# Row-wise sum of reciprocals: larger loads first, smaller loads last, and one layout of two-row chunks

## The chip, the core and the metric

The kernel runs on one core of a Trainium2 chip. The metric is the device time of one execution in microseconds (us); before the change it is 175.22 us, the median of 3 runs (174.59 to 175.49). The profile is of one execution whose span, from the first to the last instruction, is 172.6 us.

The engines are named as in the profile: PE is TensorE's matmul, PEld its weight load, DVE is VectorE, ACT is ScalarE, POOL is GpSimd, SP is SyncE, on whose queue all loads are issued here.

## What is computed

```python
x: 32 x 512 x 1024, float32, positive
return np.sum(1.0 / x, axis=-1)
```

There are 16384 rows of 1024 values. Each of the 128 partitions gets 128 consecutive rows, so in a partition the rows lie one behind the other in HBM, 4 KB each. In all 67.11 MB are read and 64 KB are written.

## The kernel before

No engine divides here. Each row is cut into halves a and b of 512 values, and the kernel uses

1/a + 1/b = (a + b) / (a b).

The reciprocal of a product is computed on ScalarE as exp(-ln(S a b)), with the constant S = 2^17 in front, which is multiplied in again at the end. This needs a logarithm and an exponential for 512 values where a row taken alone would need both for 1024.

The work is cut into groups of one or two rows (`GROUPS`, L38-L44). For each group the loop at L80 does the following.

- A load brings the group's rows into a tile xt (L82-L83). xpool has 16 such tiles of two rows. All loads are on SyncE's queue.
- The product pr = a b is formed on GpSimd (L85); in the very last group it is formed on VectorE.
- In groups marked `on_pe` (B in the code), TensorE forms the sum a + b in PSUM (L90): a matmul with an identity matrix for a, and a second one for b that is accumulated onto it. The tile is sm.
- ScalarE takes the logarithm of pr (L106) and then the exponential (L111), in place in groups B, and into a PSUM tile rc in the others (A).
- VectorE multiplies and sums in one instruction (L118). In a group A it multiplies the whole row (1024 values) by rc, which is used for both halves; in a group B it multiplies the reciprocal (512 values) by the sum in sm. An accumulator is read into `sums` after it (DVE_READ_ACCUMULATOR2).
- A group C has one row like A and a second row that ScalarE does alone: logarithm and exponential of 1024 values with the sum in its accumulator (L98, L99). There are seven such groups.

The last six groups have one row each. The order of the work on each engine is that of the framework's scheduler. At the end the 64 KB of sums are stored with one DMA (L131).

A tile goes back to its pool when the last instruction that reads or writes it has ended. In a group A that is VectorE's sum, which reads xt; in a group B the tile xt is free once GpSimd and TensorE have read it.

Of the kernel before, what the change touches and what calls it, by code (L numbers as in the profile page):

```python
# [1 line left out]

# [6 lines left out]


@with_exitstack
def kernel(
    ctx: ExitStack,
    tc: tile.TileContext,
    x: bass.AP,
    out: bass.AP,
):

    nc = tc.nc
    f32 = mybir.dt.float32
    P = 128
    D = 1024
    H = D // 2  # L30
    F = 128

    S = float(2**17)

    GP, DV = nc.gpsimd, nc.vector
    A, B, C = (2, 0, GP, False), (2, 0, GP, True), (1, 1, GP, False)  # L38
    GROUPS = (
        [A, B, A, B, C, B, A, B] * 7  # L40
        + [A, B, A, B, A]
        + [(1, 0, GP, True), (1, 0, GP, False)] * 2
        + [(1, 0, GP, True), (1, 0, DV, True)]
    )  # L44

    Ln = mybir.ActivationFunctionType.Ln
    Exp = mybir.ActivationFunctionType.Exp
    mult = mybir.AluOpType.mult
    add = mybir.AluOpType.add

    x_v = x.flatten_outer_dims().rearrange("(p f) d -> p f d", p=P)
    out_v = out.flatten().rearrange("(p f) -> p f", p=P)

    act_sets = list(get_activation_tables(nc.m.arch).keys())
    nc.scalar.add_instruction(  # L55
        mybir.InstLoadActFuncSet(
            name=nc.get_next_instruction_name(),
            act_func_set_id=act_sets.index("natural_log_exp_and_others"),
            ins=[],
            outs=[],  # L60
        )
    )

    xpool = ctx.enter_context(tc.tile_pool(name="xpool", bufs=16))
    ppool = ctx.enter_context(tc.tile_pool(name="ppool", bufs=4))
    opool = ctx.enter_context(tc.tile_pool(name="opool", bufs=1))
    rpool = ctx.enter_context(
        tc.tile_pool(name="rpool", bufs=2, space=bass.MemoryType.PSUM)
    )

    spool = ctx.enter_context(
        tc.tile_pool(name="spool", bufs=2, space=bass.MemoryType.PSUM)
    )

    sums = opool.tile([P, F], f32)
    ident = opool.tile([P, P], f32)
    make_identity(nc, ident)

    c0 = 0
    for np_, ns, eng, on_pe in GROUPS:  # L80
        n = np_ + ns
        xt = xpool.tile([P, n, D], f32, tag="xt")  # L82
        nc.sync.dma_start(out=xt, in_=x_v[:, c0 : c0 + n, :])  # L83
        pr = ppool.tile([P, np_, H], f32, tag="pr")
        eng.tensor_tensor(out=pr, in0=xt[:, :np_, :H], in1=xt[:, :np_, H:], op=mult)  # L85
        if on_pe:
            sm = spool.tile([P, np_, H], f32, tag="sm")
            for j in range(np_):
                for h in range(2):
                    nc.tensor.matmul(  # L90
                        sm[:, j, :],
                        lhsT=ident,
                        rhs=xt[:, j, h * H : (h + 1) * H],
                        start=h == 0,
                        stop=h == 1,
                    )
        for j in range(np_, n):
            nc.scalar.activation(out=xt[:, j, :], in_=xt[:, j, :], func=Ln)  # L98
            nc.scalar.activation(  # L99
                out=xt[:, j, :],  # L100
                in_=xt[:, j, :],
                func=Exp,
                scale=-1.0,
                accum_out=sums[:, c0 + j : c0 + j + 1],
            )
        nc.scalar.activation(out=pr, in_=pr, func=Ln, scale=S)  # L106
        if on_pe:
            rc = pr
        else:
            rc = rpool.tile([P, np_, H], f32, tag="rc")  # L110
        nc.scalar.activation(out=rc, in_=pr, func=Exp, scale=-1.0)  # L111
        for j in range(np_):
            if on_pe:
                row, rec = rc[:, j, :], sm[:, j, :]
            else:
                row = xt[:, j, :].rearrange("p (h e) -> p h e", h=2)
                rec = rc[:, j, :].unsqueeze(1).to_broadcast([P, 2, H])
            nc.vector.tensor_tensor_reduce(  # L118
                out=row,
                in0=row,  # L120
                in1=rec,
                scale=S,
                scalar=0.0,
                op0=mult,
                op1=add,
                accum_out=sums[:, c0 + j : c0 + j + 1],
            )
        c0 += n
    assert c0 == F, c0

    nc.sync.dma_start(out=out_v, in_=sums)  # L131


# [1 line left out]
_INS = ['x']  # L135
_OUTS = [((32, 512), 'float32')]


# [23 lines left out]
```

## Time and profile before

| | us | share of the span |
|---|---|---|
| device time | 175.22 | |
| span of the profiled execution | 172.6 | |
| POOL busy | 143.4 | 83% |
| ACT busy | 142.0 | 82% |
| PE busy | 120.9 | 70% |
| DVE busy | 109.8 | 64% |

| operation | line | count | mean of one |
|---|---|---|---|
| POOL product, two rows (128x1024) | L85 | 54 | 2365 ns |
| POOL product, one row (128x512) | L85 | 12 | 1273 ns |
| ACT logarithm, two rows | L106 | 54 | 1055 ns |
| ACT exponential into PSUM, two rows (A) | L111 | 24 | 1027 ns |
| ACT exponential in place, two rows (B) | L111 | 30 | 1056 ns |
| DVE sum of a whole row (A) | L118 | 57 | 1219 ns |
| DVE sum of a half row (B) | L118 | 64 | 685 ns |
| DVE product of one row | L85 | 1 | 689 ns |

The busy times and shares come from the first part of the page. Matmuls are counted twice there: each of the 128 in the program shows as two passes. A busy share says little by itself: the table only says that no compute engine is busy throughout. The slices, the chain and the waits say what the time is spent on; they are shown with the prediction. A group's mean in the second table is for one shape alone.

### The profile page before, as it was taken

Reading aid. Unit: us, or ns where it says so; the run is one execution under the profiler, and the core shown is the slowest. Engines: PE = TensorE matmul, PEld = TensorE weight load, DVE = VectorE, ACT = ScalarE, POOL = GpSimd, SP = SyncE. Lnnn points to the kernel's source line nnn. Section 1 sums busy time; section 2 is a strip of 40 time slices with the busy share of each in tenths; the row PEclk is TensorE's granted clock in tenths of the full one; section 3 lists DMA queues with packets and bytes.
Section 4 is the critical chain, followed back from the end, with each engine's and each line's share of the span. In section 5 each row is a group of like instructions: output and inputs, shape, how many; then the busy total and the mean of one; then the engine's idle time right before and its main releaser. Section 6 shows DMA issues by size and latency. Waiting matters only on the chain.

```text
span 172.6 us, 1342 instructions
## 1 busy us (share of the span) xinstructions
PE 120.9 (70%) x256; PEld 47.4 (27%) x256; DVE 109.8 (64%) x243; ACT 142.0 (82%) x156; POOL 143.4 (83%) x72
## 2 busy tenths in 40 slices
PE   0099776767876767788666668977667876669480
PEld 0043322222332222233322223422222332223130
DVE  0009757874776757775578847468576755787791
ACT  2159989899878998889888996889988898988981
POOL 1599699969989799987999688997999979999920
PEclk9999999999999999999999996999999999999999
DMA  5999999999999999999999999999999999999500
GB/s 190 416 433 425 423 420 423 421 421 423 418 425 420 423 418 423 423 420 423 421 421 420 423 414 423 421 420 420 425 418 425 425 420 421 421 412 408 220 0 15
DMA packets 9799, 67.25 MB, mean 390 GB/s; under 512 B 1088, under 2 KB 1216, under 8 KB 1984
## 3 DMA queue, kind: packets, MB, share of 16 engines
q1 hardware_dynamic: 9792, 67.18, 94.0%
q8 instruction: 2, 0.03, 0.1%
q14 instruction: 5, 0.04, 0.1%
HBM read 67.11 MB, written 0.07 MB: 389 GB/s over the span
## 4 chain that ended last, share of the span: by engine, by line
DMA 78%; POOL 11%; ACT 2%; issue 2%; DVE 2%; SPq 1%; PE 1%; POOLq 0%; DVEq 0%
DMA xt<-in_x_dram 78%; POOL pr L85 11%; SPq L83 1%; ACT pr L106 1%; PE sm L90 1%; DVE xt L118 1%; ACT rc L111 1%; DVE pr L118 0%; ACT pr L111 0%; DVE pr L85 0%; POOLq L85 0%; DVE sums L118 0%; DVEq L118 0%; DVEq L157 0%
## 5 line engine op out<-in xcount | busy, mean ns | idle before, releaser
L85 POOL TENSOR_TENSOR pr<-xt 128x1024 f32<-128x1024 f32 (+1 forms) x66 | 142.7, 2166 | 21.1 <-DMA xt<-in_x_dram 15.2
L90 PE MATMUL sm<-xt,ident 128*128 128x512 f32 x256 | 120.9, 617 | 47.0 <-DMA xt<-in_x_dram 45.0
L118 DVE CUSTOM_DVE_ANT_1 xt<-xt,rc 128x1024 f32<-128x1024 f32 x57 | 67.7, 1219 | 50.2 <-issue 27.2
L106 ACT ACTIVATE pr<-pr 128x1024 f32<-128x1024 f32 (+1 forms) x67 | 65.0, 970 | 24.5 <-POOL pr L85 23.7
L90 PEld LDWEIGHTS sm<-xt,ident 128*128 128x128 f32 x256 | 47.4, 195 | 119.7 <-issue 57.8
L118 DVE CUSTOM_DVE_ANT_0 pr<-pr,sm 128x512 f32<-128x512 f32 x64 | 41.6, 685 | 9.8 <-ACT pr L111 8.6
L111 ACT ACTIVATE pr<-pr 128x1024 f32<-128x1024 f32 (+1 forms) x34 | 34.2, 1006 | 1.0
L111 ACT ACTIVATE rc<-pr 128x1024 f32<-128x1024 f32 (+1 forms) x33 | 29.9, 906 | 0.8
L118 DVE DVE_READ_ACCUMULATOR2_ANT sums<- 128x1 f32 x121 | 10.0, 82 | 0.0
L99 ACT ACTIVATE xt<-xt 128x1024 f32<-128x1024 f32 x7 | 7.3, 1041 | 0.0
L98 ACT ACTIVATE xt<-xt 128x1024 f32<-128x1024 f32 x7 | 7.3, 1040 | 0.0
L55 ACT ACT_TABLE_LOAD x1 | 1.3, 1283 | 0.7 <-PEq L146 0.7
L99 ACT ACTIVATION_READ_ACCUMULATOR xt<-xt 128x1 f32 x7 | 1.3, 186 | 0.0
L85 DVE TENSOR_TENSOR pr<-xt 128x512 f32<-128x512 f32 x1 | 0.7, 689 | 0.0
masks.py:197 POOL MEMSET ident<- 128x128 f32 x1 | 0.2, 204 | 0.3 <-POOLq L146 0.3
masks.py:199 POOL TENSOR_SCALAR_AFFINE_SELECT ident<-ident 128x128 f32<-128x128 f32 x1 | 0.3, 292 | 0.1
L146 POOL MEMSET const-float32-0.0<- 128x1 f32 x1 | 0.1, 98 | 0.2 <-issue 0.2
L146 POOL MEMSET const-bfloat16-1.0<- 128x1 bf16 x1 | 0.1, 101 | 0.0
L146 POOL MEMSET const-uint8-127<- 128x1 uint8 x1 | 0.1, 101 | 0.0
L146 POOL MEMSET const-float32-1.0<- 128x1 f32 x1 | 0.1, 98 | 0.0
## 6 DMA issues: line engine op xcount, KB each, us to landing
xt<-in_x_dram SPq DMA_DIRECT2D x61, 1024.0 KB, 19.8
xt<-in_x_dram SPq DMA_DIRECT2D x6, 512.0 KB, 15.6
out_dram<-sums SPq DMA_DIRECT2D x1, 64.0 KB, 1.5
```

Of the source, the lines that this page charges most:

```text
L55: nc.scalar.add_instruction(mybir.InstLoadActFuncSet(name=nc.get_next_instruction_name(), act_func_set_id=act_sets.index("natural_log_exp_ ...
L83: nc.sync.dma_start(out=xt, in_=x_v[:, c0 : c0 + n, :])
L85: eng.tensor_tensor(out=pr, in0=xt[:, :np_, :H], in1=xt[:, :np_, H:], op=mult)
L90: nc.tensor.matmul(sm[:, j, :], lhsT=ident, rhs=xt[:, j, h * H : (h + 1) * H], start=h == 0, stop=h == 1,)
L98: nc.scalar.activation(out=xt[:, j, :], in_=xt[:, j, :], func=Ln)
L99: nc.scalar.activation(out=xt[:, j, :], in_=xt[:, j, :], func=Exp, scale=-1.0, accum_out=sums[:, c0 + j : c0 + j + 1],)
L106: nc.scalar.activation(out=pr, in_=pr, func=Ln, scale=S)
L111: nc.scalar.activation(out=rc, in_=pr, func=Exp, scale=-1.0)
L118: nc.vector.tensor_tensor_reduce(out=row, in0=row, in1=rec, scale=S, scalar=0.0, op0=mult, op1=add, accum_out=sums[:, c0 + j : c0 + j + 1],)
L146: nc = _bacc.Bacc("TRN2", target_bir_lowering=False, num_devices=1)
```

## The change

The change replaces the mixture of groups by chunks of two rows and takes several chunks with one load.

- A load brings eight rows (8 loads), then four rows (12 loads), then two rows (8 loads): 28 loads in place of 67. Per partition a load is one run of 32, 16 or 8 KB. The large tiles come from xpool (4 tiles of eight rows), the two-row tiles from a pool of their own, epool (4 tiles).
- All chunks have two rows. A is as before. B has the halves added on TensorE, as before. C is like B, but the product of its first row is formed on VectorE, from b as TensorE has copied it to PSUM (a matmul with the identity) and a in SBUF. C is every fourth chunk, so this is every eighth product. No row is done on ScalarE alone any more.
- The order on each engine is fixed to that of the program (`keep`). The sums of a chunk are issued one chunk later (`waiting`), behind the products of the next chunk. A C chunk's product on VectorE stands at the head of its load.
- The pools change: ppool has 6 tiles for 4. In PSUM there are three tiles of one row for the sums, one for b, and two of two rows for rc.

It is meant to have fewer and longer transfers, shares that suit the engines, and short pieces at the end.

```diff
-    A, B, C = (2, 0, GP, False), (2, 0, GP, True), (1, 1, GP, False)
-    GROUPS = (
-        [A, B, A, B, C, B, A, B] * 7
-        + [A, B, A, B, A]
-        + [(1, 0, GP, True), (1, 0, GP, False)] * 2
-        + [(1, 0, GP, True), (1, 0, DV, True)]
-    )
+    A, B, C = (2, 0, 0), (2, 2, 0), (2, 2, 1)
+    LOADS = [[A, B, A, C]] * 8 + [[A, B], [A, C]] * 6 + [[A], [B], [A], [C]] * 2
...
-    xpool = ctx.enter_context(tc.tile_pool(name="xpool", bufs=16))
-    ppool = ctx.enter_context(tc.tile_pool(name="ppool", bufs=4))
+    xpool = ctx.enter_context(tc.tile_pool(name="xpool", bufs=4))
+    epool = ctx.enter_context(tc.tile_pool(name="epool", bufs=4))
+    ppool = ctx.enter_context(tc.tile_pool(name="ppool", bufs=6))
...
+    for chunks in LOADS:
+        n = sum(m for m, _, _ in chunks)
+        if n > 2:
+            xt = xpool.tile([P, n, D], f32, tag="xt")
         else:
+            xt = epool.tile([P, n, D], f32, tag="xe")
+        keep(nc.sync.dma_start(out=xt, in_=x_v[:, c0 : c0 + n, :]))
+
+        made, q = [], 0
+        for m, e, v in chunks:
+            pr = ppool.tile([P, m, H], f32, tag="pr")
+            for j in range(v):
+                b = bpool.tile([P, H], f32, tag="b")
+                add(b, xt[:, q + j, H:])
+                i = nc.vector.tensor_tensor(
+                    out=pr[:, j, :], in0=xt[:, q + j, :H], in1=b, op=mult
+                )
+                keep(i)
...
+        for (m, e, v), pr in zip(chunks, made):
+            xc = xt[:, q : q + m, :]
+            if v < m:
+                i = nc.gpsimd.tensor_tensor(
+                    out=pr[:, v:, :], in0=xc[:, v:, :H], in1=xc[:, v:, H:], op=mult
+                )
+                keep(i)
+            sm = []
+            for j in range(e):
+                s = spool.tile([P, H], f32, tag="s")
+                add(s, xc[:, j, :H], xc[:, j, H:])
+                sm.append(s)
+            if waiting:
+                sum_rows(*waiting)
+            keep(nc.scalar.activation(out=pr, in_=pr, func=Ln, scale=S))
...
+            waiting = c0 + q, xc, pr, sm, rc
...
+    sum_rows(*waiting)
```

More of the change, by code (lines that the diff above doesn't have):

```diff
@@ L33 @@
     S = float(2**17)
-    GP, DV = nc.gpsimd, nc.vector
-    A, B, C = (2, 0, GP, False), (2, 0, GP, True), (1, 1, GP, False)
-    GROUPS = (
-        [A, B, A, B, C, B, A, B] * 7
-        + [A, B, A, B, A]
-        + [(1, 0, GP, True), (1, 0, GP, False)] * 2
-        + [(1, 0, GP, True), (1, 0, DV, True)]
-    )
+    A, B, C = (2, 0, 0), (2, 2, 0), (2, 2, 1)
+    LOADS = [[A, B, A, C]] * 8 + [[A, B], [A, C]] * 6 + [[A], [B], [A], [C]] * 2
     Ln = mybir.ActivationFunctionType.Ln
@@ L48 @@
     mult = mybir.AluOpType.mult
-    add = mybir.AluOpType.add
+    plus = mybir.AluOpType.add
     x_v = x.flatten_outer_dims().rearrange("(p f) d -> p f d", p=P)
@@ L62 @@
     )
-    xpool = ctx.enter_context(tc.tile_pool(name="xpool", bufs=16))
-    ppool = ctx.enter_context(tc.tile_pool(name="ppool", bufs=4))
+    xpool = ctx.enter_context(tc.tile_pool(name="xpool", bufs=4))
+    epool = ctx.enter_context(tc.tile_pool(name="epool", bufs=4))
+    ppool = ctx.enter_context(tc.tile_pool(name="ppool", bufs=6))
     opool = ctx.enter_context(tc.tile_pool(name="opool", bufs=1))
+    spool = ctx.enter_context(
+        tc.tile_pool(name="spool", bufs=3, space=bass.MemoryType.PSUM)
+    )
+    bpool = ctx.enter_context(
+        tc.tile_pool(name="bpool", bufs=1, space=bass.MemoryType.PSUM)
+    )
     rpool = ctx.enter_context(
         tc.tile_pool(name="rpool", bufs=2, space=bass.MemoryType.PSUM)
-    )
-    spool = ctx.enter_context(
-        tc.tile_pool(name="spool", bufs=2, space=bass.MemoryType.PSUM)
     )
@@ L77 @@
     make_identity(nc, ident)
-    c0 = 0
[L80 to L108, printed above, removed]
-        else:
[L110 to L127, printed above, removed]
@@ new lines, with add, sum_row @@
+    keep = tc.keep_in_program_order
+    def add(bank, *halves):
+        for k, half in enumerate(halves):
+            i = nc.tensor.matmul(
+                bank,
+                lhsT=ident,
+                rhs=half,
+                start=k == 0,
+                stop=k == len(halves) - 1,
+            )
+            keep(i)
+    def sum_row(c, row, fac):
+        i = nc.vector.tensor_tensor_reduce(
+            out=row,
+            in0=row,
+            in1=fac,
+            scale=S,
+            scalar=0.0,
+            op0=mult,
+            op1=plus,
+            accum_out=sums[:, c : c + 1],
+        )
+        keep(i)
@@ new lines, in sum_rows @@
+    def sum_rows(c, xc, pr, sm, rc):
+        m, e = xc.shape[1], len(sm)
+        for j in range(e, m):
+            row = xc[:, j, :].rearrange("p (h e) -> p h e", h=2)
+            sum_row(c + j, row, rc[:, j - e, :].unsqueeze(1).to_broadcast([P, 2, H]))
+        for j in range(e):
+            sum_row(c + j, pr[:, j, :], sm[j])
+    waiting = None
+    c0 = 0
+    for chunks in LOADS:
+        n = sum(m for m, _, _ in chunks)
+        if n > 2:
+            xt = xpool.tile([P, n, D], f32, tag="xt")
+        else:
+            xt = epool.tile([P, n, D], f32, tag="xe")
[8 more added lines that the diff above has]
+                    out=pr[:, j, :], in0=xt[:, q + j, :H], in1=b, op=mult
+                )
+                keep(i)
+            made.append(pr)
+            q += m
+        q = 0
+        for (m, e, v), pr in zip(chunks, made):
[3 more added lines that the diff above has]
+                    out=pr[:, v:, :], in0=xc[:, v:, :H], in1=xc[:, v:, H:], op=mult
+                )
+                keep(i)
+            sm = []
+            for j in range(e):
+                s = spool.tile([P, H], f32, tag="s")
[4 more added lines that the diff above has]
+            keep(nc.scalar.activation(out=pr, in_=pr, func=Ln, scale=S))
+            rc = None
+            if e < m:
+                rc = rpool.tile([P, m - e, H], f32, tag="rc")
+                i = nc.scalar.activation(
+                    out=rc, in_=pr[:, e:, :], func=Exp, scale=-1.0
+                )
+                keep(i)
+            if e:
+                r = pr[:, :e, :]
+                keep(nc.scalar.activation(out=r, in_=r, func=Exp, scale=-1.0))
+            waiting = c0 + q, xc, pr, sm, rc
+            q += m
```

## The prediction

> **What bounds the kernel now.** I read the slices of the page first (is any resource full all the time?), then the chain of waits, then the DMA issues and the waits of the DMA queue, then the last 20 us.
>
> ```profile
> PE 120.9 (70%) x256; PEld 47.4 (27%) x256; DVE 109.8 (64%) x243; ACT 142.0 (82%) x156; POOL 143.4 (83%) x72
> ...
> DMA  5999999999999999999999999999999999999500
> ...
> q1 hardware_dynamic: 9792, 67.18, 94.0%
> ...
> DMA 78%; POOL 11%; ACT 2%; issue 2%; DVE 2%; SPq 1%; PE 1%; POOLq 0%; DVEq 0%
> ...
> xt<-in_x_dram SPq DMA_DIRECT2D x61, 1024.0 KB, 19.8
> xt<-in_x_dram SPq DMA_DIRECT2D x6, 512.0 KB, 15.6
> out_dram<-sums SPq DMA_DIRECT2D x1, 64.0 KB, 1.5
> ```
>
> The DMA row is full from the second slice to the third from last, and 78% of the chain is loads. No compute engine is full. The DMA queue's waits say how the loads are spaced:
>
> ```profile
> SPq L83 <- DMA xt<-in_x_dram: 123.4, 59, 2.6
> ```
>
> 59 of 67 loads waited for an earlier load to land, so eight are in flight. A load takes 19.8 us from issue to landing behind seven others, so one lands each 19.8/8 = 2.48 us. The sixteen tiles of xpool never ran short. The windows give the rate for the two sizes, and the end:
>
> ```profile
> 10.00:152.00 142.00, 107.42 (x230) 42.39 (x229) 95.33 (x211) 124.72 (x135) 125.98 (x58) 0.99 1.01 422
> 154.50:160.50 6.00, 5.28 (x13) 1.97 (x12) 4.13 (x10) 5.20 (x6) 5.90 (x4) 1.00 1.02 409
> 163.50:164.50 1.00, 0.29 (x1) 0.29 (x2) 1.00 (x5) 0.97 (x2) 1.00 (x2) 1.00 0.08 16
> 164.50:165.50 1.00, 1.00 (x3) 0.39 (x3) 1.00 (x3) 0.97 (x3) 0.57 (x1) 1.00 0.00 0
> ```
>
> Runs of 8 KB per partition flow at 422 GB/s, the 4 KB runs of the last six loads at 409. The last bytes arrive at about 164.0. The last sum ends at 169.8 and the span at 172.6: 5.8 us of compute behind the last load, then 2.8 us for the output. So the time is when the last load lands, plus 8.6 us, plus 2.6 us that the span doesn't hold (175.22 - 172.6).
>
> **What the Trainium skill says.** "DMA: Bandwidth & Descriptors", Specifications, gives a fabric ceiling of 435 GB/s; the 422 here agrees, and caps what longer runs can bring at 3%. The same page, Anatomy of one DMA, puts a fixed cost of about 2 us on each DMA, mostly completion. Here the first load takes 4.8 us (the minimum from issue to landing), 2.3 beyond its own 2.48 us; the 64 KB output takes 1.5 in all. It is hidden while other loads are queued, and is paid when the queue runs dry. "SBUF — State Buffer", A bandwidth-pool intuition that's wrong, says that GpSimd and a two-port VectorE operation exclude each other; the change reads b from PSUM, and no run here shows the conflict. "PSUM — Partial Sum Buffer", Specifications, has eight banks of 2 KiB; the new pools take 3 + 1 + 4, so they fit.
>
> **The change part by part.** All engine work first, by the present rows. GpSimd: the new kernel has 48 products of two rows (2365 ns) and 16 of one (1273 ns), 113.5 + 20.4 = 133.9 us for 142.7. ScalarE: the seven rows that it did alone go (7 x (1040 + 1041 + 186) = 15.9 us); 64 chunks cost 64 x 1.055 + 32 x 1.027 + 32 x 1.056 + 1.3 = 135.5 us for 142.0. VectorE: seven more full rows, 7 x (1.22 + 0.08), and 16 products at 0.69 (the one there is now; b in PSUM I take at the same price, between 0.61, the step between half-row sums that read PSUM, and 0.75 with a gap): 109.8 + 9.1 + 11.0 = 130 us. TensorE: 16 more matmuls, two passes each at 0.472 (120.9/256): 136 us. Each stays below the 157 us that the loads need, so all of this is hidden and costs nothing.
>
> Larger loads. The queue's 9792 packets are 67 x 128 rows, 128 for the output and 68 x 16 = 1088 small ones: a load is eight data packets on each of 16 DMA engines. By the rates a load of 1 MB takes 2.485 us and one of 512 KB 1.282, so the part that doesn't grow is 2 x 1.282 - 2.485 = 0.08 us. That would make the bytes alone run at 436 GB/s, just over the ceiling, and the 409 was read where some DMA engines were ending, so I take 0.056, seven tenths. 67 loads become 28: 39 x 0.056 = 2.2 us gained, between 0 and 3.1. A four-row load is then about 4.92 us, an eight-row one 9.78. That the first load lands at about 12.6 instead of 5.5 costs nothing if compute catches up.
>
> Does it? Per eight rows GpSimd needs 3 x 2.49 (its spacing in the chain's last 20 us) + 1.4 = 8.9 us and the loads bring eight in 9.8. After the last eight-row load it is 3.95 us late (8.87 - 4.92); each pair of four-row loads takes 0.96 us off, and at the twelfth it is level. That load needs 3.9 us and the next two-row load comes after 2.5: **GpSimd starts the two-row loads 1.45 us late**.
>
> Buffers. A chunk A holds its rows until VectorE has summed them. Its time is in these rows, for the product that GpSimd begins at 151.56:
>
> ```profile
> 153.97 1.06 ACT L106 ACTIVATE pr<-pr 128x1024 f32<-128x1024 f32 x1 [0.35 <-POOL pr L85]
> 155.06 1.03 ACT L111 ACTIVATE rc<-pr 128x1024 f32<-128x1024 f32 x1
> ...
> 156.21 1.22 DVE L118 CUSTOM_DVE_ANT_1 xt<-xt,rc 128x1024 f32<-128x1024 f32 x1 [1.26 <-issue]
> ...
> 157.36 1.22 DVE L118 CUSTOM_DVE_ANT_1 xt<-xt,rc 128x1024 f32<-128x1024 f32 x1
> ```
>
> 158.58 - 151.56 = 7.0 us. An eight-row load is given back 3 x 2.49 + 4.7 = 12.2 us after landing, with three more (29 us) queued. The first four-row loads are tightest: 12.2 + 7.2 until the fourth could land, against 4 x 4.92 = 19.7. No gap, by 0.2 us.
>
> The two-row loads have four tiles for eight loads. Call them e1 to e8 and count from e1's landing. In the program as built, e5 takes e2's tile (it waits for GpSimd and TensorE), e6 takes e1's, e7 e3's, e8 e4's; the loads issue in this order on one queue, so what waits behind e7 is e8. GpSimd ends e2 at 1.5 + 2 x 2.49 = 6.5: e5 is issued there, when the queue (e4 ends at 6.9) is nearly dry. GpSimd begins e3 at 6.6, so its sums end at 13.6 and **e7 is issued at 13.6**. Its data start 1.0 to 1.7 us later (the 1.6 before the first load's bytes, less for a warm queue), at 14.6 to 15.3. With the queue never dry, e7 would start at 6.9 + 2 x 2.48 = 11.8. So the loads stand still for 2.8 to 3.5 us, middle 3.15, all of it on the path.
>
> Behind e8's landing: GpSimd is through with e7, ScalarE runs e7's two steps (2.1) and e8's two (2.1) and VectorE e8's two half-row sums (1.4 with the wait): 5.7. e8's product of b (matmuls 1.0, product 0.7) lies beside e7's steps. As now, 5.8.
>
> Sum: 175.2 - 2.2 + 3.15 = **176.2 us**.
>
> **The rivals.** (1) The queue refills faster, or GpSimd isn't late: e3's sums end at 5.0 + 7.1 = 12.1, data start 0.7 later, and the gap is 1.0. With 3.1 gained by long packets: 175.2 - 3.1 + 1.0 = 173.1; with one of the two, about 174. For it speaks the output's 1.5 us, against it that the 1.45 us come from three rows of the present trace. (2) Long packets bring nothing (HBM sets 422): 175.2 + 3.5 = 178.7, or 178.3 at the middle. Against it speaks 409 against 422; for it, that no packet above 8 KB is in the trace. (3) The seven microseconds at the start are never recovered, because small waits on ordered queues (VectorE's product for the next load stands ahead of the last chunk's sums) make a chunk as dear as its load: 175.2 + 7 = 182. Against it: 0.9 us of slack in each eight rows.
>
> **How the numbers follow.** Forecast 42%, rival (1) 28%, (2) 25%, (3) 5%. The range runs from 173.0, which takes in nearly all of (1), to 178.8, which takes in (2) and leaves out (3) and a little at each end. The forecast lies on the edge of half a per cent (176.1): half of it counts as the same, half as slower. (1) counts as faster, (2) and (3) as slower: faster 0.28, same 0.21, slower 0.51.
>
> **What would show it.** Windows in the first 80 us above 422 GB/s (429 by my price) for the packets; DMA slices full up to about 140 us, then a hole of 3 us, with the DMA queue waiting for VectorE ahead of e7; GpSimd idle about 1 us at each eight-row load; the chain ending through ScalarE and VectorE about 5.8 us behind the last landing. A DMA row without the hole, or 422 in the first windows, would prove a step wrong.

## The result, and the profile after

The changed kernel takes **177.39 us** (median of 4 runs, 177.01 to 177.96) for 174.97 us before on the same chip: ratio 1.014, with a 95% interval of 1.010 to 1.018. It is slower by 2.4 us. The profiled execution spans 175.3 us, the one before 172.6. All times in this document are of executions in the chip's usual state; one of all, 182.99 us in the run with b from SBUF, fell into a slower one and is left out.

From the page of the changed kernel: busy times, the slices of the DMA engines and their GB/s, and the loads.

```profile
PE 137.4 (78%) x288; PEld 53.2 (30%) x288; DVE 125.0 (71%) x272; ACT 133.9 (76%) x129; POOL 133.1 (76%) x70
...
DMA  6999999999999999999999999999999999579800
GB/s 202 441 434 426 426 449 441 411 441 441 435 419 434 441 422 419 435 441 396 430 422 340 400 336 426 426 441 441 419 426 419 441 411 421 215 245 350 364 0 15
...
xt<-in_x_dram SPq DMA_DIRECT2D x8, 4096.0 KB, 27.7
xt<-in_x_dram SPq DMA_DIRECT2D x12, 2048.0 KB, 12.3
xt<-in_x_dram SPq DMA_DIRECT2D x8, 1024.0 KB, 11.3
```

The busy times are near those that the prediction worked out (GpSimd 133.9 predicted, 133.1 here; ScalarE 135.5 and 133.9; VectorE 130 and 125; TensorE 136 and 137), and none is the bound. The GB/s row tells the story: about 430 for the first half, a dip (340, 400, 336) in the slices from 92 to 105 us, and a hole (215, 245) in the two slices from 149 to 158 us. The DMA row itself shows only the second.

The waits of the DMA queue of the changed kernel (who was waited for, us in all, times, longest):

```profile
SPq L119 <- DVE sums L91: 125.0, 18, 22.1
SPq L119 <- PE s L81: 20.2, 1, 20.2
```

Before, the queue waited for loads to land (59 times), that is, only because enough were in flight. Now it waits for VectorE, and once for TensorE, to give a tile back. A long wait here costs nothing as long as other loads are queued behind the DMA engines; it costs where they run dry. The windows show where (stretch, length, TensorE's clock, busy share of the DMA engines, GB/s):

```profile
20.00:80.00 60.00, 1.00 1.00 432
...
92.00:96.00 4.00, 1.00 0.90 348
96.00:100.00 4.00, 1.00 0.89 365
100.00:104.00 4.00, 1.00 1.00 348
104.00:150.00 46.00, 1.00 1.00 426
150.00:155.00 5.00, 1.00 0.34 123
155.00:157.00 2.00, 1.00 0.91 332
157.00:159.00 2.00, 1.00 1.00 303
159.00:165.00 6.00, 0.80 1.01 411
```

Long runs do flow faster, 432 for 422 GB/s. Then there are two gaps, one at the step from eight-row to four-row loads, one among the two-row loads, and behind both the stream comes back below its rate: 348 GB/s at 100 to 104 us and 303 at 157 to 159, though the DMA share is 1.00 in both. The two-row loads are called e1 to e8 as in the prediction, and "#4" is the fourth four-row load.

The second gap, instruction by instruction (timeline of the changed kernel; in brackets the idle time and what ended it):

```profile
151.70 1.98 PE L81 MATMUL s<-xt,ident 128*128 128x512 f32 x4 [0.64 <-DVE sums L91]
...
153.75 5.90 SPq L119 DMA_DIRECT2D xt<-in_x_dram  x3
...
158.64 2.36 POOL L138 TENSOR_TENSOR pr<-xt 128x1024 f32<-128x1024 f32 x1 [2.80 <-DMA xt<-in_x_dram]
162.02 6.22 POOL L138 TENSOR_TENSOR pr<-xt 128x1024 f32<-128x1024 f32 x3 [1.02 <-DMA xt<-in_x_dram]
```

TensorE reads e2's second row until 153.68, e5 is issued into that tile at 153.75 and lands at 158.5, 4.8 us later, as long as the first load of the kernel before took on an empty queue (4.8). GpSimd stands idle for 2.8 us. e6 lands 3.4 us after e5, not 2.48. The last sum ends at 172.7 and the span 2.6 us after it.

A landing is told here by the last of the 16 DMA engines that share a load. By the trace the engines drift apart: e4's landings reach from 151.2 on the first to 153.7 on the last. Most engines therefore had nothing to move from about 151.5, well before e5 was issued, until its data started at 154.7.

### The profile page after: what moved, and what is told of

Read it like the earlier page. It is cut to its first block, busy times and chain, and to the rows that moved or that the text cites. A ratio compares the mean times of both kernels' runs of the same rounds, so it can differ in the third digit from the quotient of the medians.

```text
span 175.3 us, 1332 instructions
## 1 busy us (share of the span) xinstructions
PE 137.4 (78%) x288; PEld 53.2 (30%) x288; DVE 125.0 (71%) x272; ACT 133.9 (76%) x129; POOL 133.1 (76%) x70
## 5 line engine op out<-in xcount | busy, mean ns | idle before, releaser
L138 POOL TENSOR_TENSOR pr<-xt 128x1024 f32<-128x1024 f32 x64 | 132.4, 2098 | 34.6 <-DMA xt<-in_x_dram 34.3
L81 PE MATMUL s<-xt,ident 128*128 128x512 f32 x256 | 122.7, 618 | 18.1 <-DVE sums L91 13.9
L91 DVE CUSTOM_DVE_ANT_1 xt<-xt,rc 128x1024 f32<-128x1024 f32 x64 | 75.6, 1219 | 30.4 <-ACT rc L153 21.6
L149 ACT ACTIVATE pr<-pr 128x1024 f32<-128x1024 f32 x64 | 67.3, 1052 | 34.6 <-POOL pr L138 34.2
L81 PEld LDWEIGHTS s<-xt,ident 128*128 128x128 f32 x256 | 47.9, 195 | 91.1 <-issue 55.9
L91 DVE CUSTOM_DVE_ANT_0 pr<-pr,s 128x512 f32<-128x512 f32 x64 | 41.4, 682 | 1.1 <-ACT pr L159 0.9
L159 ACT ACTIVATE pr<-pr 128x1024 f32<-128x1024 f32 x32 | 33.8, 1058 | 1.0
L153 ACT ACTIVATE rc<-pr 128x1024 f32<-128x1024 f32 x32 | 32.9, 1028 | 1.0
L81 PE MATMUL b<-xt,ident 128*128 128x512 f32 x32 | 18.4, 658 | 16.1 <-DMA xt<-in_x_dram 16.0
L127 DVE TENSOR_TENSOR pr<-xt,b 128x512 f32<-128x512 f32 x16 | 10.9, 684 | 16.3 <-PE b L81 16.2
L81 PEld LDWEIGHTS b<-xt,ident 128*128 128x128 f32 x32 | 5.4, 196 | 26.5 <-issue 15.2
```

The lines of the kernel that those rows point to most:

```text
L81: i = nc.tensor.matmul(bank, lhsT=ident, rhs=half, start=k == 0, stop=k == len(halves) - 1,)
L91: i = nc.vector.tensor_tensor_reduce(out=row, in0=row, in1=fac, scale=S, scalar=0.0, op0=mult, op1=plus, accum_out=sums[:, c : c + 1],)
L127: i = nc.vector.tensor_tensor(out=pr[:, j, :], in0=xt[:, q + j, :H], in1=b, op=mult)
L138: i = nc.gpsimd.tensor_tensor(out=pr[:, v:, :], in0=xc[:, v:, :H], in1=xc[:, v:, H:], op=mult)
L149: keep(nc.scalar.activation(out=pr, in_=pr, func=Ln, scale=S))
L153: i = nc.scalar.activation(out=rc, in_=pr[:, e:, :], func=Exp, scale=-1.0)
```

## The experiments

Each kernel was timed beside the kernel before on the same chip. The medians of the kernel before lay between 174.8 and 175.1 us. The changed kernel itself was timed apart from them, so differences from its 177.39 us carry the spread of that measurement too (ratio 1.010 to 1.018). In the code, "..." stands for lines left out.

### Late tiles: away with the second gap

```diff
-        if n > 2:
+        if n > 2 or c0 >= F - 8:
             xt = xpool.tile([P, n, D], f32, tag="xt")
```

> The changed kernel, but the last four two-row loads (e5 to e8) take tiles of the large pool, which are long free, in place of the four tiles of the small pool. Theory (the loads stand still because e5 and e6 wait for a tile): the hole of 3.15 us before e5 and e6 is gone and GpSimd, which is late there anyway, gives 0.3 back: about 174.5 us, all DMA slices full to the end. Rival (compute is late at the end and the hole only mirrors it): the loads land earlier, the end does not move: 177 us or more.

Measured: 173.67 us, ratio 0.992 (0.990 to 0.995). The second gap is gone: the windows of 150 to 160 us show 419 GB/s throughout, and the time falls by 3.7 us, 0.8 more than expected. This one line turns the change from slower to faster than before. The rival is out: the end follows the loads.

### Four-row loads from the start

```diff
-    LOADS = [[A, B, A, C]] * 8 + [[A, B], [A, C]] * 6 + [[A], [B], [A], [C]] * 2
+    LOADS = [[A, B], [A, C]] * 14 + [[A], [B], [A], [C]] * 2
...
-    xpool = ctx.enter_context(tc.tile_pool(name="xpool", bufs=4))
+    xpool = ctx.enter_context(tc.tile_pool(name="xpool", bufs=8))
```

> The changed kernel, but its eight loads of eight rows become sixteen of four (eight tiles of four rows, the same memory); the end with two-row loads stays as it is. Theory (the step from eight to four rows makes a hole, since four large tiles hold only four small loads): the hole between 94 and 103 us is gone (1.1 us on the DMA engine that lands last), runs of 16 KB in place of 32 KB cost 8 x (2 x 4.89 - 9.71) = 0.6 us, and the hole before e5 stays: about 176.9 us. Rival (what costs is that compute starts seven us later behind a 4 MB load): compute starts about 5 us earlier, and the time falls to 173 us or less.

Measured: 176.48 us (175.51 to 177.52), ratio 1.009 (1.006 to 1.012), 0.9 below the changed kernel and 0.4 below what was expected; the two intervals overlap a little. The dip at 92 to 105 us is gone (its page shows 414 to 434 GB/s there), the gap among the two-row loads is still there. The rival's 173 us is far off: the late start of compute behind a 4 MB load isn't what costs.

### Two-row loads throughout

```diff
-    LOADS = [[A, B, A, C]] * 8 + [[A, B], [A, C]] * 6 + [[A], [B], [A], [C]] * 2
+    LOADS = [[A], [B], [A], [C]] * 16
...
-    epool = ctx.enter_context(tc.tile_pool(name="epool", bufs=4))
+    epool = ctx.enter_context(tc.tile_pool(name="epool", bufs=20))
```

> The changed kernel with all loads of two rows (64 loads, twenty tiles): the chunks and the engines' shares of the change without its loads. Theory (long runs gain, holes cost): the stream takes 64 x 2.485 = 159.0 us for 156.2, plus 2.8, and both holes go, minus 4.2: about 175.5 us, the time of the kernel before, and windows at 422 GB/s. Rival (the length of the runs is worth nothing): only the holes go, 173.2 us.

Measured: 174.73 us, ratio 0.998 (0.997 to 1.000), the time of the kernel before. So the new chunks, their order and their shares of the engines by themselves are worth nothing: they change what is hidden. (The sum hides two small differences: the profiled span is 0.4 us longer, 173.0 for 172.6, and the part of the time outside the span is as much shorter, 1.8 us for 2.2.) Its window shows the rate of short runs again, as the kernel before has it:

```profile
20.00:80.00 60.00, 1.00 1.01 421
```

### b from SBUF

```diff
...
-                b = bpool.tile([P, H], f32, tag="b")
-                add(b, xt[:, q + j, H:])
                 i = nc.vector.tensor_tensor(
-                    out=pr[:, j, :], in0=xt[:, q + j, :H], in1=b, op=mult
+                    out=pr[:, j, :], in0=xt[:, q + j, :H], in1=xt[:, q + j, H:], op=mult
                 )
```

> The changed kernel, but every eighth product on VectorE reads b where it lies in SBUF: no copy by TensorE to PSUM. Theory (VectorE and TensorE have time to spare, GpSimd works beside them undisturbed): the same within 0.5 us, 177.4, GpSimd's two-row product still 2365 ns. Rival (VectorE with two inputs in SBUF and GpSimd exclude each other): GpSimd's products that meet one of the sixteen are up to 0.7 us longer, and the time is 178 us.

Measured: 178.76 us (178.28 to 179.68, three executions), ratio 1.020 (1.016 to 1.025), 1.4 us above the changed kernel, whose interval it overlaps. The theory missed on the instructions, and the rival named the wrong victim. Groups by line and shape (count, busy us, mean ns), first of the changed kernel, then of this run:

```profile
L138 POOL TENSOR_TENSOR pr<-xt 128x1024 f32<-128x1024 f32 x48 | 112.7, 2371 | 34.4 <-DMA xt<-in_x_dram 34.3
...
L127 DVE TENSOR_TENSOR pr<-xt,b 128x512 f32<-128x512 f32 x16 | 10.9, 684 | 16.3 <-PE b L81 16.2
```

```profile
L133 POOL TENSOR_TENSOR pr<-xt 128x1024 f32<-128x1024 f32 x48 | 116.7, 2453 | 30.5 <-DMA xt<-in_x_dram 27.3 <-ACT rc L148 3.0
...
L122 DVE TENSOR_TENSOR pr<-xt 128x512 f32<-128x512 f32 x16 | 24.1, 1509 | 13.6 <-DMA xt<-in_x_dram 13.6
L133 POOL TENSOR_TENSOR pr<-xt 128x512 f32<-128x512 f32 x16 | 23.1, 1445 | 0.1
```

VectorE's product takes 1509 ns in the mean for 684, up to 2873: one that meets a GpSimd product stands until that is through. The longest begins at 25.69 us, 0.02 us after a GpSimd product that ends at 28.02, and ends itself at 28.57; the GpSimd product behind it takes 2.8 us. In the mean GpSimd loses less (2453 for 2371, and 1445 for 1279 on one row). This agrees with what the Trainium skill says in "SBUF — State Buffer", SBUF: two separate sides: a VectorE operation with two inputs in SBUF and a GpSimd operation that reads SBUF lock each other out for a whole instruction.

That the added time comes from this lock isn't shown. In this build e5 waits for e1's tile, which VectorE gives back, and no longer for e2's, which TensorE gives back; the queue's waits show it:

```profile
SPq L116 <- DVE sums L88: 144.6, 18, 22.7
SPq L116 <- PE s L78: 2.8, 3, 1.4
```

e5 is issued 8.9 us after e1's landing for 7.4 in the changed kernel. That is 1.4 us, as much as the whole difference, and e1's tile is free 8.8 us after its landing in both runs. What the copy of b to PSUM is worth by itself stays open.

### Both gaps away

The four-row loads and the late tiles together:

> The changed kernel with both holes taken away at once: four-row loads from the start (as in the run with four-row loads) and tiles of the large pool for the last four two-row loads (as in the run with late tiles). Theory (the two holes are separate and add up): 177.4 - 3.7 - 0.9, the two measured steps, = 172.8 us; DMA slices full from the second to the end. Rival (the stretch of compute behind the loads takes over once one hole is gone): no better than 173.7, the time with the late tiles alone.

Measured: 172.99 us, ratio 0.990 (0.987 to 0.992). The two steps add up within 0.2 us, so the two losses are separate. Its rate is between the others:

```profile
20.00:80.00 60.00, 1.00 1.00 427
```

### A tile for the transition

The late tiles with the eight-row loads kept, and a tile of its own for #4:

```diff
+    mpool = ctx.enter_context(tc.tile_pool(name="mpool", bufs=1))
...
-        if n > 2 or c0 >= F - 8:
+        if c0 == 76:
+            xt = mpool.tile([P, n, D], f32, tag="xm")
+        elif n > 2 or c0 >= F - 8:
             xt = xpool.tile([P, n, D], f32, tag="xt")
```

> The run with late tiles (e5 to e8 in the large pool), and one more tile of four rows that the fourth four-row load takes, so that it waits for nobody; the eight-row loads stay. Theory (the hole at 94 us is the fourth four-row load's wait for the last eight-row tile): that hole goes, the time falls from 173.7 by about 1.1 to 172.6 us. Rival (the hole comes from the DMA side, where the loads change their size): it stays, 173.7.

Measured: **172.54 us**, ratio 0.987 (0.984 to 0.989), 1.1 below the run with late tiles. The dip is gone with the wait; the loads still change their size there. This version beats both kernels. Its windows:

```profile
20.00:80.00 60.00, 1.00 1.00 431
...
92.00:96.00 4.00, 1.00 1.02 434
96.00:100.00 4.00, 1.00 0.99 422
100.00:104.00 4.00, 1.00 1.02 426
```

### A quicker end, and a lighter one

> Four-row loads and late tiles as in the first run of this set, and a lighter end: the last two four-row loads are A and C, then three times A and C of two rows, then four loads of one row (product on GpSimd, VectorE, GpSimd, VectorE by way of PSUM, the second and fourth with halves added on TensorE). Theory (5.9 us from the last landing to the last sum are two rows' worth of ScalarE and VectorE work, and GpSimd is late by 0.3): the end takes about 4.9 us, the short loads cost 0.1: 0.9 below the first run, about 172.0 us. Rival (the fixed part of each instruction on one row eats the gain): the same as the first run.

Measured: 173.14 us for 172.99: the rival's time, so loads of one row at the end bring nothing here. That it is the fixed part of each instruction that eats the gain isn't shown.

> The run with the transition tile, and C in place of B in the last two four-row loads and in all two-row loads, so that GpSimd forms 3 products in 4 rows of the end instead of 7 in 8. Theory (GpSimd is 1.5 us late when the two-row loads begin, and part of the 5.9 us behind the last landing is that): up to 0.4 us less, 172.2. Rival (the end is two rows' worth of ScalarE and VectorE work whatever GpSimd does): 172.5, no change.

Measured: 172.53 us for 172.54. Less work for GpSimd at the end changes nothing either. In its trace e8 lands at 162.2; ScalarE then works without a pause on two steps for e7 and two for e8 until 166.5, and VectorE's last sums end at 168.1: the 5.9 us are those of ScalarE and VectorE, as the prediction had them.

### The kernel before with eight-row loads

```diff
...
+        if c0 < 112:
+            if c0 % 8 == 0:
+                xb = xpool.tile([P, 8, D], f32, tag="xt")
+                nc.sync.dma_start(out=xb, in_=x_v[:, c0 : c0 + 8, :])
+            xt = xb[:, c0 % 8 : c0 % 8 + n, :]
...
```

> The kernel before with its groups, engines and shares untouched, but the first 112 rows come in 14 loads of eight rows (four tiles of eight), the last 16 rows as before (seven small tiles, the last four loads in large ones). Theory (long runs gain 3.2 us of stream, but GpSimd's 54 x 2.47 + 12 x 1.37 = 149.8 us then start at 13.5 and cannot end before 163.3): the end moves by at most 1.7 us, 173.4 to 175.0, with GpSimd never waiting for long. Rival (the stream alone sets the time): 171.8 us.

Measured: 177.34 us, ratio 1.014 (1.012 to 1.017): slower, beyond both expectations. The stream gains what it should (the last load lands at 160.9 for 164.0), and the gain is lost behind it. Windows of this run (PE, PEld, DVE, ACT, POOL busy, clock, DMA share, GB/s) and the last row of GpSimd's timeline:

```profile
157.00:161.00 4.00, 3.05 (x8) 1.17 (x7) 2.93 (x7) 3.97 (x5) 4.00 (x2) 1.00 0.51 205
161.00:162.00 1.00, 1.00 (x3) 0.19 (x1) 1.00 (x3) 1.00 (x2) 1.00 (x2) 1.00 0.00 0
162.00:165.00 3.00, 1.48 (x4) 0.68 (x4) 2.72 (x7) 2.94 (x5) 3.00 (x3) 1.00 0.00 0
...
149.73 17.85 POOL L93 TENSOR_TENSOR pr<-xt 128x1024 f32<-128x1024 f32 x10
```

All loads have landed by 161, but GpSimd works without a pause from 149.7 to 167.6. The theory had its earliest end at 163.3, and took it that GpSimd would never wait for long. It waited 11 us for loads after the first one (23.3 in all, 12.2 before it could begin): an eight-row load holds 8.3 to 9.3 us of its work and the next comes only after 9.7, and it can't work ahead. When the last eight-row load is there (141.1), GpSimd still has 26.5 us of work before it, and the loads are through in 20. The changed kernel has long loads too and doesn't pay this, as the run with a tile for the transition shows. It has less work for GpSimd, a fixed order, and four-row loads between the long ones and the short; which of these it is, no run separates.

### Five small tiles, and six

```diff
-    epool = ctx.enter_context(tc.tile_pool(name="epool", bufs=4))
+    epool = ctx.enter_context(tc.tile_pool(name="epool", bufs=5))
```

> The changed kernel with five tiles in the small pool for four. Now e5 has a free tile, e6 waits for e2's, e7 for e1's, e8 for e3's. By the changed kernel's trace e2 is free 7.4 us after e1's landing, e1 after 8.7 and e3 after 13.0. Theory (the hole is the wait for a tile plus 1.0 to 2.4 us until data flow again): e6's data start at 8.4 to 9.8 where the queue runs dry at 9.3, e8's at 14.0 to 15.4 for 14.3: a hole of 0 to 1.5 us in place of 3.2, about 174.4 us. Rival (one tile more of five changes little, the loads wait in a row): 176.5 us or more.

Measured: 177.48 us (175.48 to 177.96), ratio 1.013 (1.006 to 1.019): a miss. The waits are shorter, as worked out, and the median is that of four tiles, though one of the four executions took 2 us less. Timeline of the profiled one, the slowest (177.96):

```profile
153.52 5.91 SPq L119 DMA_DIRECT2D xt<-in_x_dram  x3
...
158.59 3.67 PE L81 MATMUL s<-xt,ident 128*128 128x512 f32 x8 [0.45 <-DMA xt<-in_x_dram]
162.35 2.36 POOL L138 TENSOR_TENSOR pr<-xt 128x1024 f32<-128x1024 f32 x1 [1.35 <-DMA xt<-in_x_dram]
166.57 1.26 POOL L138 TENSOR_TENSOR pr<-xt 128x512 f32<-128x512 f32 x1 [1.87 <-DMA xt<-in_x_dram]
```

e6 is issued at 153.5 and e8, the third of these issues, at 159.1. The rows that wait for e6, e7 and e8 start at 158.6, 162.3 and 166.6: e7 and e8 land 3.8 and 4.2 us after the one ahead, though both were issued before that one landed. By the trace part of this is a single DMA engine: e8 lands on 15 of them by 165.1 and on the last at 166.4. Another part is compute: e8 comes so late that its own product no longer lies beside e7's steps, and the last sum ends 7.1 us behind the last landing for 5.9 in the changed kernel.

> The changed kernel with six tiles in the small pool for four: e5 and e6 have free tiles, e7 takes e2's (free 7.4 us after e1's landing, its data are due at 11.8), e8 takes e1's (free at 8.7, due at 14.3). With five tiles the time did not move (177.5), although only short waits were left; there the loads after the first short gap landed 3.8 and 4.2 us apart in place of 2.5. Theory A (any gap, even a short one, is paid again by slow loads behind it; without a gap nothing is paid): no hole at all and 173.7 us, the time with the late tiles. Theory B (the small pool is the cost, whatever its waits): 176.5 us or more. Theory C (the wait itself is the cost, in proportion): with five tiles it should have fallen by half, so 173.7 here would leave the five-tile run unexplained.

Measured: 173.73 us, ratio 0.993 (0.989 to 0.996), the time with the late tiles (173.67). So the small pool by itself isn't the cost (theory B is out), and without a wait nothing is paid, as theory A has it. The medians look like all or nothing: four tiles 177.4, five 177.5, six 173.7. But with five tiles one execution lies at 175.5, about where theory C would have it, and the slow one has the losses just named, so that a short gap always costs as much as a long one isn't shown. DMA slices of the run with six:

```profile
DMA  6999999999999999999999899999999999999600
```

Why a gap is paid again behind it is not settled. In the traces with a gap, the first 8 KB packets behind it take 0.4 to 1.0 us on nearly all DMA engines at once (0.31 is their median), and in the changed kernel the first packets of e6, one load later, take 1.2 to 1.35. What slows them, no run isolates.

## Why the prediction was right, and where not

Forecast 176.2 us and slower, from a gain of 2.2 and a loss of 3.15; measured 2.4 us slower, where 1.0 was forecast. The direction and the two main terms were right; a third term, the step to four-row loads, was set at nothing and cost 1.1 us, and that the loss of 3.15 came out near was in part luck, as it arose in another place. By its steps:

- **Loads set the time, engine work is hidden.** Shown for the new chunks: two-row loads with all the new chunks take 174.73 for 174.78.
- **28 loads for 67 gain 2.2 us.** Shown, where nothing spoils it: 174.73 with two-row loads, 172.54 with eight, four and two rows and no gap, 2.2 us for 36 loads fewer, where the price of 0.056 us a load gives 2.0. The price itself was too low: loads of two, four and eight rows land 2.485, 4.89 and 9.71 us apart, so each load saved is worth 0.07 to 0.08, as the prediction had it before it took seven tenths. That the sum still came out is luck; why not all of it reaches the end isn't settled. The windows read 421, 427 and 432 GB/s for runs of 8 KB, mostly 16 KB and 32 KB, where 429 was forecast for the first 80 us. Rival (2), that HBM sets 422, is out.
- **The first four-row loads: "No gap, by 0.2 us".** This step failed. The last eight-row tile was given back at 94.6, 11.9 us after its landing (12.2 predicted), and #4 was issued at 94.75, yet the flow dipped to 348 GB/s. The sum was nearly right for the last of the 16 DMA engines: #4 lands only 0.3 us later than it would in an unbroken stream. But the sum took the queue as one. The landings of the last eight-row load are 2.3 us apart from the first engine to the last, so most engines ran dry before #4's data came. And it had nothing for what follows a gap: #5 lands 5.7 us behind #4 for 4.9. The two delays make the 1.1 us that the run with a tile for #4 wins back (173.67 less 172.54).
- **A gap of 3.15 us among the two-row loads.** The size was nearly right (3.7 by the time with late tiles), the route was not. The prediction has e5 issued 6.5 us after e1's landing and charges nothing for it, though its own figures (queue dry at 6.9, data 1.0 to 1.7 us behind the issue) leave a gap of 0.6 to 1.3 there; the load that comes late is e7. In the trace e5 waits until 153.75, 7.4 us after e1's landing: e2's second sum on TensorE had to wait for VectorE to free one of three PSUM tiles. Its data start 1.0 us behind the issue, as taken, but most engines had been dry since 151.5, 5.2 us after e1's landing and not 6.9. e5 lands 4.8 us behind e4, 2.3 more than its own flow, just what the prediction had read from the first load and not used here; e6 lands another 0.9 late: 3.2 us. e7 is issued at 159.33, close to the forecast, but by then the stream is so far behind that it costs nothing more. The gap of 1.0 us of rival (1) did not come.
- **GpSimd starts the two-row loads 1.45 us late.** Right by the trace (e1 lands at 146.3, GpSimd begins on it at 147.6, 1.2 us late), and without weight where the gaps are gone: with a lighter end the time stays.
- **5.8 us behind the last landing.** Right: the last load lands at 166.8 and the last sum ends at 172.7. The 2.6 us that the span doesn't hold were taken from a median and a span of different executions. The profiled execution before took 174.78 us, 2.2 beyond its span, and that of the changed kernel 177.13, 1.8 beyond it. So inside the span the change costs 2.7 us, and 0.4 comes back outside it, for a reason that no run shows.
- **Rival (3), a start that is never recovered**: no in the changed kernel (four-row loads start earlier and gain 0.9, no more than the dip's 1.1, and eight-row loads without gaps beat the kernel before), yes in the kernel before with eight-row loads.

In sum: 174.7 - 2.2 (long runs) + 1.1 (transition) + 3.7 (two-row loads) = 177.3 us. This closes by its making, since each term is a difference of two of these runs. What tests it is the run with both gaps away: 172.8 from the single steps, 172.99 measured.

## What to carry to other kernels

Where loads set the time, count for each step in their size how long the tile that the next load needs is still held, against what is queued ahead of it. Count to the first DMA engine that runs dry (here some 2 us ahead of the last), and leave microseconds, not tenths, because in these traces a gap was paid again by the load behind it. A pool for the small pieces at the end should hold them all, or take tiles that the large loads have done with. A larger load makes compute start later and lands its work in larger lots: the kernel before lost more by that than the longer runs gave it.

## What the runs showed of the hardware

- A load on an empty queue took 4.8 us from issue to landing, at the start of the kernel before and in mid-stream (e5), for 2.48 us of its own flow.
- A DMA queue that ran dry did not come back at its rate: in the changed kernel 303 to 332 GB/s in the 4 us behind the gap for 426 ahead of it, and a load of 1 MB landed 3.4 us behind the one ahead for 2.48.
- The 16 DMA engines drift apart in a long stream: the landings of one load were 0.4 us apart for the first load of the kernel before and 2.2 for the last.
- A VectorE product with both inputs in SBUF took 1.5 us in the mean and up to 2.9 beside GpSimd's products, for 0.68 with one input in PSUM; GpSimd's two-row product took 2.45 for 2.37.
- Runs of 32 KB in HBM and SBUF came in at 432 GB/s, those of 8 KB at 421.
